# Holding GpSimd's first weight splits behind a juncture until the second half's sums of squares instead of the first half's

## The chip, the cores and the metric

One core of one Trainium2 chip runs the whole program. The metric is the device time of one execution in microseconds (us), as the median of several runs; smaller is better.

## The reference, cut to what matters

A sequence of 512 tokens of width 1024 goes through two attention layers (`first_block`) and then twice through FFN, token mixer, FFN (`second_block`). Each of these eight branches is normalised before and after and added to the stream:

```python
h = rms_norm(x, pre_norm[l]); proj = h @ w_in[l]
...
y = concatenate([oa, ob, om]) @ w_out[l]
x = x + rms_norm(y, post_norm[l])
...
h = swiglu(rms_norm_2(x, g[0]), ffn_w_in[layer, 0], ffn_w_out[layer, 0])
x = x + 0.5 * rms_norm_2(h, g[1])
h = token_mixer(rms_norm_2(x, g[2]), mix_w_in[layer], ...)
x = x + rms_norm_2(h, g[3])
```

All data is float32. `rms_norm` needs the sum of squares over all 1024 channels of a token.

## The kernel before, in words

**Layout.** The stream `XT` lies with channels on the partitions: 8 chunks of 128 channels by 512 tokens. Tokens are taken in two halves of 256 (`HALF`). Every float32 product is made of three matmuls of rounded parts: `mm3` (L353, L354, L355) multiplies high by high, high by low and low by high. So each weight tile is loaded (`wr`, L395, two buffers, 512 KB each), its high part is cast on ScalarE (`wh`, L419), and its low part, the difference, is made by GpSimd (`wl`, L421): one such *split* is 128x512, and a tile has two of them. A third tile can be loaded only when the two splits of the first have read their `wr`.

**A juncture** is where one branch ends and the next begins; seven of the eight ends have a next branch. Class `Join` does it: for each half `t` it waits for the norm of the branch's output (`scale`, `spread`), and then for each pair `i` of channel chunks runs `front(t, i)` and `back(t, i)`. `front` scales the output (VectorE L281, or L285 twice where a gain `gpost` is left to apply), adds it to the stream (VectorE L287), makes the next branch's high parts `xh` (ScalarE, L289, two), squares the pair (ScalarE L495) and lets GpSimd add the squares to `sacc` (`square2`: L498 once for the first pair, L501 twice for each other). `back` makes the low parts `xl` (VectorE L299, two), which read `XT` and `xh`. Four junctures end in an output projection (`gpost` is None: they begin near 344, 655, 1368 and 2456 us of the span); I call them *plain*. Three end an FFN (near 1030, 1746 and 2118 us), with `gpost`.

**Lead.** The next branch begins with `lead`: with weights that VectorE has already split, TensorE multiplies the two first units for half 0 (`run(0)`) and then for half 1 (`run(1)`), 32 `mm3` each. During `run(1)`, after 12 of them, it sums `sacc` over the partitions (`ss_matmul`, L473), VectorE makes the inverse root r of half 0 (`rsqrt`: nine instructions L364 to L372 on 128x2 values, each waiting for the one before), and after 18 more TensorE spreads r (`col_bcast`, L438), ScalarE copies it to `R` (L536), and VectorE scales the results (`evac`). The same is done for half 1 some `mm3` into the next unit. TensorE's order is fixed: a spread that has no r yet stops it.

**The gate.** The weights after the lead are split by GpSimd (`wload`, `wsplit`). Their program order is late, but the scheduler may place them early. `k.gate` holds the first 8 of them back: `behind` (L398) makes them stand behind a named GpSimd instruction in GpSimd's order.

```python
added = k.square2(k.pre[t], i, x)
if (t, i) == (0, 3):
    k.gate = [added, 8]
```

Of the kernel before, what the change touches and what calls it, by code (L numbers as in the profile page):

```python
# [210 lines left out]
class Join:  # L211
# [60 lines left out]
    def front(self, t, i):  # L272

        k, nc, put = self.k, self.nc, self.put
        v = nc.vector
        sl, c = HALF[t], slice(2 * i, 2 * i + 2)
        if t not in self.scratch:
            self.scratch[t] = (k.mm if t else k.sc)().rearrange("p (a n) -> p a n", a=2)
        s, P = self.scratch[t], self.P[t]
        if self.gpost is None:  # L280
            put(v.tensor_tensor(s, self.Y[:, c, sl], P[:, None, :].to_broadcast([128, 2, 256]), op=OP.mult))  # L281
        else:
            for e in range(2):
                j = 2 * i + e
                put(v.scalar_tensor_tensor(s[:, e], self.Y[:, j, sl], self.gpost[:, j:j + 1], P, op0=OP.mult, op1=OP.mult))  # L285
        x = k.XT[:, c, sl]
        put(v.tensor_tensor(x, x, s, op=OP.add))  # L287
        for j in (2 * i, 2 * i + 1):
            nc.scalar.activation(k.h[0][:, j, sl], k.XT[:, j, sl], AF.Copy, scale=k.gcol(self.nxt[0], j))  # L289
        added = k.square2(k.pre[t], i, x)  # L290
        if (t, i) == (0, 3):
            k.gate = [added, 8]

    def back(self, t, i):
# [1318 lines left out]
```

## Time and profile before

| | |
|---|---|
| median of 3 runs | 2847.77 us (2847.34 to 2848.65) |
| profiled execution, its own time | 2845.98 us |
| its span, first to last instruction | 2844.0 us |
| granted TensorE clock, mean | 0.992 |
| busy: TensorE matmul, VectorE, ScalarE, GpSimd | 2741.8, 1412.6, 1374.1, 1356.5 us |

The times in the trace are microseconds from the start of the span. A line such as `L421` is a line of the kernel; `[1.20 <-DVE xl L299]` means that the engine was idle for 1.20 us and that VectorE's instruction on `xl` ended that.

### The profile page before, as it was taken

The numbers are of one execution on the slowest core, as the hardware profiler recorded it, in microseconds if no ns is written. First come the engines' busy times: TensorE is split into PE (matmuls) and PEld (weight loads), VectorE is DVE, ScalarE is ACT, GpSimd is POOL, SyncE is SP. The second block draws the span as 40 slices with busy tenths as digits, with TensorE's granted clock in tenths as the row PEclk, the third lists the DMA queues.
The fourth block names the chain that finished last, engine by engine and source line by source line (L and its number), as shares of the span: only waits on it lengthen the run. The fifth ranks groups of instructions, "written<-read, shape, count | busy, mean of one in ns | idle before, by whom it ended". The sixth has DMA issues, their size and how long they took to land.

```text
span 2844.0 us, 42873 instructions
## 1 busy us (share of the span) xinstructions
PE 2741.8 (96%) x16080; PEld 2398.0 (84%) x16080; DVE 1412.6 (50%) x2988; ACT 1374.1 (48%) x2881; POOL 1356.5 (48%) x1327
## 2 busy tenths in 40 slices
PE   8999999999999999899999999999998899999998
PEld 8997899788888887898988888888887798888887
DVE  6589757986302266747630225312336747731132
ACT  5678547874333335657433334333334758433332
POOL 4553365424444455443544445444455543544545
PEclk9999999999999999999999999999999999999999
DMA  5111221112333222121223232233222120223332
GB/s 176 60 46 38 75 72 46 45 66 75 96 92 103 85 81 83 51 79 62 78 96 96 97 93 93 89 89 104 95 77 86 62 81 31 90 82 91 105 99 77
DMA packets 69280, 230.53 MB, mean 81 GB/s; under 512 B 8968, under 2 KB 11912, under 8 KB 68816
## 3 DMA queue, kind: packets, MB, share of 16 engines
q1 hardware_dynamic: 69072, 227.78, 24.5%
q8 instruction: 127, 2.08, 0.3%
q14 instruction: 81, 0.66, 0.1%
HBM read 225.51 MB, written 2.24 MB: 80 GB/s over the span
## 4 chain that ended last, share of the span: by engine, by line
PE 74%; DVE 15%; ACT 4%; issue 3%; POOL 2%; DMA 2%; SPq 0%; POOLq 0%; DVEq 0%; ACTq 0%
PE sc L354 11%; PE sc L353 11%; PE sc L355 11%; PE mm L355 11%; PE mm L353 11%; PE mm L354 11%; DVE xl L299 2%; PE sc L116 2%; PE tp L145 1%; DVE pl L149 1%; DVE XT L287 1%; DVE nm L192 1%; DVE E L204 1%; PE tp L817 1%; POOL wl L421 1%
## 5 line engine op out<-in xcount | busy, mean ns | idle before, releaser
L421 POOL TENSOR_TENSOR wl<-wr,wh 128x512 fp32r<-128x512 f32 x732 | 942.0, 1297 | 883.0 <-ACT wh L419 858.9
L419 ACT CAST wh<-wr 128x512 fp32r<-128x512 f32 x836 | 500.5, 612 | 722.8 <-PE sc L354 450.9
L354 PE MATMUL sc<-xl,wh 128*128 128x512 f32 (+1 forms) x1824 | 658.0, 361 | 16.3 <-DVE xl L299 16.2
L355 PE MATMUL sc<-xh,wl 128*128 128x512 f32 (+1 forms) x1824 | 654.5, 359 | 0.2 <-DVE wl L421 0.2
L353 PE MATMUL sc<-xh,wh 128*128 128x512 f32 (+1 forms) x1824 | 653.2, 360 | 0.0
L607 DVE TENSOR_TENSOR fg<-sc,R 128x512 f32<-128x512 f32 (+1 forms) x92 | 59.3, 644 | 747.6 <-PE sc L355 724.5
L354 PEld LDWEIGHTS sc<-xl,wh 128*128 128x128 f32 x1824 | 344.0, 189 | 72.1 <-DVE xl L299 20.7
L355 PEld LDWEIGHTS sc<-xh,wl 128*128 128x128 f32 x1824 | 344.2, 189 | 51.8 <-DVE wl L421 0.4
L353 PEld LDWEIGHTS sc<-xh,wh 128*128 128x128 f32 x1824 | 342.5, 189 | 51.5
L355 PE MATMUL mm<-ah,wl 128*128 128x512 f32 (+1 forms) x792 | 291.0, 367 | 6.5 <-POOL wl L421 6.5
L353 PE MATMUL mm<-ah,wh 128*128 128x512 f32 (+1 forms) x792 | 290.3, 367 | 1.9 <-ACT wh L419 1.9
L354 PE MATMUL mm<-al,wh 128*128 128x512 f32 (+1 forms) x792 | 289.3, 365 | 0.0
L353 PE MATMUL mm<-wh,xh 128*128 128x256 f32 x960 | 275.0, 286 | 0.0
L354 PE MATMUL mm<-wl,xh 128*128 128x256 f32 x960 | 273.2, 285 | 0.0
L355 PE MATMUL mm<-wh,xl 128*128 128x256 f32 x960 | 273.0, 284 | 0.0
L353 PE MATMUL mm<-xh,wh 128*128 128x512 f32 (+1 forms) x560 | 196.7, 353 | 10.5 <-DVE big L789 3.4
L355 PE MATMUL mm<-xh,wl 128*128 128x512 f32 (+1 forms) x560 | 194.8, 348 | 7.8 <-POOL wl L421 7.8
L354 PE MATMUL mm<-xl,wh 128*128 128x512 f32 (+1 forms) x560 | 193.9, 346 | 0.0
L354 PEld LDWEIGHTS mm<-wl,xh 128*128 128x128 f32 x960 | 184.1, 192 | 1.3
L353 PEld LDWEIGHTS mm<-wh,xh 128*128 128x128 f32 x960 | 183.9, 192 | 1.0
L355 PEld LDWEIGHTS mm<-wh,xl 128*128 128x128 f32 x960 | 184.0, 192 | 0.9
L355 PEld LDWEIGHTS mm<-ah,wl 128*128 128x128 f32 x792 | 149.2, 188 | 33.8 <-POOL wl L421 9.6
(348 smaller groups left out, 4878.1 us busy)
## 6 DMA issues: line engine op xcount, KB each, us to landing
wr<-in_ffn_in_dram SPq DMA_DIRECT2D x176, 512.0 KB, 3.3
wr<-in_ffn_out_dram SPq DMA_DIRECT2D x64, 512.0 KB, 3.6
wr<-in_mix_in_dram SPq DMA_DIRECT2D x56, 512.0 KB, 3.3
wr<-in_w_in_dram SPq DMA_DIRECT2D x48, 512.0 KB, 3.3
wr<-in_ffn_out_dram SPq DMA_DIRECT2D x32, 384.0 KB, 3.1
wr<-in_w_out_dram SPq DMA_DIRECT2D x16, 512.0 KB, 3.3
wr<-in_mix_out_dram SPq DMA_DIRECT2D x16, 512.0 KB, 3.3
Mb<-Md SPq DMA_DIRECT2D x16, 256.0 KB, 3.1
```

Of the source, the lines that this page charges most:

```text
L116: nc.tensor.matmul(sc[:, e], q, kk[:, :n], start=j == 0, stop=j == len(self.K) - 1)
L145: nc.tensor.transpose(p[:, j * per + e], E[i + e][:, j * 128:(j + 1) * 128], self.k.ident)
L149: nc.vector.tensor_tensor(pl[:, :nk, sl], pv, ph[:, :nk, sl].bitcast(F32), op=OP.subtract)
L192: nc.vector.tensor_reduce(nm, sc, axis=AX.X, op=OP.max, negate=True)
L204: nc.vector.scalar_tensor_tensor(E[tb, 0], E[tb, 1], cc[:, i:i + 1], E[tb, 0], op0=OP.mult, op1=OP.add)
L299: self.put(self.nc.vector.scalar_tensor_tensor(lo, k.XT[:, j, sl], k.gcol(self.nxt[0], j), hi.bitcast(F32), op0=OP.mult, op1=OP.subtract))
L353: mm(out, lhs[0], rhs[0], start=start, stop=False, skip_group_check=shared)
L354: mm(out, lhs[0], rhs[1], start=False, stop=False, skip_group_check=shared)
L355: mm(out, lhs[1], rhs[0], start=False, stop=stop, skip_group_check=shared)
L419: nc.scalar.copy(hi[:, :m], raw[:, c:c + m])
L421: ins = eng.tensor_tensor(low[:, :m], raw[:, c:c + m], hi[:, :m].bitcast(F32), op=OP.subtract)
L607: nc.vector.tensor_tensor(g, ps[0], R[:, sl], op=OP.mult)
```

## The change

The gate is set by the last sum of the second half instead of the last sum of the first half. The number of splits that it holds (8) stays.

```diff
         added = k.square2(k.pre[t], i, x)
-        if (t, i) == (0, 3):
+        if (t, i) == (1, 3):
             k.gate = [added, 8]
```

The scheduler then orders GpSimd and ScalarE otherwise; TensorE's order is the same row for row, and VectorE's differs by one pair of rows elsewhere.

GpSimd, second juncture (attention to FFN, 655 us). `sacc` of L498 and L501 are the sums of squares, `wl` the splits:

```order
 L501 TENSOR_TENSOR sacc<-sacc,sq 128x256 x4
-L421 TENSOR_TENSOR wl<-wr,wh 128x512 x4
-L498 TENSOR_TENSOR sacc<-sq 128x256
-L501 TENSOR_TENSOR sacc<-sacc,sq 128x256 x2
-L421 TENSOR_TENSOR wl<-wr,wh 128x512 x2
-L501 TENSOR_TENSOR sacc<-sacc,sq 128x256 x4
-L421 TENSOR_TENSOR wl<-wr,wh 128x512 x35
+L498 TENSOR_TENSOR sacc<-sq 128x256
+L501 TENSOR_TENSOR sacc<-sacc,sq 128x256 x6
+L421 TENSOR_TENSOR wl<-wr,wh 128x512 x41
```

Four splits stood in front of the second half's first sums and two more in the midst of them; now all of that half's seven sums come first, and the splits follow in one row. The other six junctures change in the same way.

ScalarE, third juncture (FFN to mixer, 1030 us). `xh` and `sq` are the pairs of the second half, `wh` the casts, `R` the copy of the spread r:

```order
 L495 ACTIVATE sq<-XT 128x512
-L419 CAST wh<-wr 128x512 x2
 L289 ACTIVATE xh<-XT,gains 128x256 x2
 L495 ACTIVATE sq<-XT 128x512
```

and a few rows on, at the copy of r:

```order
 L495 ACTIVATE sq<-XT 128x512
 L536 COPY R<-tp 128x256
-L419 CAST wh<-wr 128x512
+L419 CAST wh<-wr 128x512 x3
 L536 COPY R<-tp 128x256
```

The two casts of the third weight tile stood between the second half's pairs; now they stand behind the first copy of r. In the plain junctures one or two casts of that tile now stand right in front of that copy.

## Rows read from the trace of the kernel before

**Rows 1.** The page's first part: busy time of each engine, share, instructions.

```profile
PE 2741.8 (96%) x16080; PEld 2398.0 (84%) x16080; DVE 1412.6 (50%) x2988; ACT 1374.1 (48%) x2881; POOL 1356.5 (48%) x1327
```

**Rows 2.** Waits of TensorE over the span: us in total, times, longest us.

```profile
PE sc L354 <- DVE xl L299: 16.2, 21, 1.3
```

**Rows 3.** Timeline, GpSimd, second juncture (plain): start, us, instruction, count, idle before.

```profile
672.46 5.38 POOL L421 TENSOR_TENSOR wl<-wr,wh 128x512 fp32r<-128x512 f32 x4
677.80 0.91 POOL L498 TENSOR_TENSOR sacc<-sq 128x256 f32<-128x256 f32 x1
...
683.08 3.57 POOL L501 TENSOR_TENSOR sacc<-sacc,sq 128x256 f32<-128x256 f32 x4
```

**Rows 4.** Timeline, VectorE, same juncture: low parts and the chain for r.

```profile
667.08 0.88 DVE L299 SCALAR_TENSOR_TENSOR xl<-XT,gains,xh 128x256 fp32r<-128x256 f32 x2 [0.58 <-ACT xh L289]
...
675.47 2.64 DVE L299 SCALAR_TENSOR_TENSOR xl<-XT,gains,xh 128x256 fp32r<-128x256 f32 x2
...
679.36 1.36 DVE L299 SCALAR_TENSOR_TENSOR xl<-XT,gains,xh 128x256 fp32r<-128x256 f32 x2
...
681.96 4.09 DVE L299 SCALAR_TENSOR_TENSOR xl<-XT,gains,xh 128x256 fp32r<-128x256 f32 x4
685.97 0.15 DVE L364 TENSOR_SCALAR rnx<-tp 128x2 f32<-128x2 f32 x1
...
687.88 0.16 DVE L372 SCALAR_TENSOR_TENSOR r<-rnt,r 128x2 f32<-128x2 f32 x1
```

**Rows 5.** Timeline, TensorE, same juncture: two waits and the spread of r.

```profile
676.74 0.38 PE L354 MATMUL sc<-xl,wh 128*128 128x256 f32 x1 [1.20 <-DVE xl L299]
...
683.47 0.39 PE L354 MATMUL sc<-xl,wh 128*128 128x256 f32 x1 [0.43 <-DVE xl L299]
...
688.49 0.38 PE L438 MATMUL tp<-ident,r 128*128 128x128 f32 x2
```

**Rows 6.** Timeline, ScalarE, same juncture: third weight tile's casts, copy of r.

```profile
678.48 1.14 ACT L419 CAST wh<-wr 128x512 fp32r<-128x512 f32 x2 [1.46 <-DMA wr<-in_ffn_in_dram]
...
688.90 0.37 ACT L536 COPY R<-tp 128x256 f32<-128x256 f32 x1 [4.36 <-PE tp L438]
```

**Rows 7.** Timeline, VectorE, third juncture (FFN to mixer): low parts, end of r.

```profile
1047.52 2.73 DVE L299 SCALAR_TENSOR_TENSOR xl<-XT,gains,xh 128x256 fp32r<-128x256 f32 x2
...
1051.81 2.37 DVE L299 SCALAR_TENSOR_TENSOR xl<-XT,gains,xh 128x256 fp32r<-128x256 f32 x2
...
1060.29 0.16 DVE L372 SCALAR_TENSOR_TENSOR r<-rnt,r 128x2 f32<-128x2 f32 x1
```

**Rows 8.** Timeline, GpSimd, third juncture: its last two sums.

```profile
1057.43 1.63 POOL L501 TENSOR_TENSOR sacc<-sacc,sq 128x256 f32<-128x256 f32 x2 [0.53 <-ACT sq L495]
```

**Rows 9.** Timeline, TensorE, third juncture: first wait and the spread of r.

```profile
1048.87 0.39 PE L354 MATMUL sc<-xl,wh 128*128 128x256 f32 x1 [1.34 <-DVE xl L299]
...
1061.37 0.38 PE L438 MATMUL tp<-ident,r 128*128 128x128 f32 x2
```

**Rows 10.** Timelines of GpSimd and VectorE at the program's start.

```profile
57.90 2.54 POOL L421 TENSOR_TENSOR wl<-wr,wh 128x512 fp32r<-128x512 f32 x2 [1.63 <-ACT wh L419]
...
58.78 0.43 DVE L365 TENSOR_SCALAR r<-rnx 128x2 int32<-128x2 int32 x1
59.25 1.21 DVE L366 TENSOR_TENSOR rnt<-r 128x2 f32<-128x2 f32 x1
```

**Rows 11.** View of line L367: ns min/median/max, first and last start, shapes.

```profile
L367 DVE SCALAR_TENSOR_TENSOR rnt<-rnt,rnx x33: 160/160/163, 24.8 to 2834.1; 128x2 f32<-128x2 f32 x33
```

**Rows 12.** Timelines, VectorE and TensorE: half 1's r, first and third juncture.

```profile
382.06 0.16 DVE L372 SCALAR_TENSOR_TENSOR r<-rnt,r 128x2 f32<-128x2 f32 x1
...
383.10 0.38 PE L438 MATMUL tp<-ident,r 128*128 128x128 f32 x2
...
1065.13 0.16 DVE L372 SCALAR_TENSOR_TENSOR r<-rnt,r 128x2 f32<-128x2 f32 x1
...
1066.22 0.38 PE L438 MATMUL tp<-ident,r 128*128 128x128 f32 x2
```

## The prediction

> **What bounds the kernel now.** I began with the busy times: TensorE's matmuls fill 96% of the span [rows 1], so a change counts only where it makes TensorE stop, or no longer stop. The list of TensorE's waits comes next. Its first line is the wait of the lead's matmuls for VectorE's low parts: 16.2 us in 21 waits, three for each of the seven junctures [rows 2]. This change touches those junctures only, so I then read the timelines of one plain juncture (the second) and one behind an FFN (the third).
>
> In the second, four splits run on GpSimd from 672.46 us for 5.38 us, ahead of half 1's first sum [rows 3]. In that time VectorE's first two low parts take 2.64 us; the same two take 0.88 us when GpSimd is idle [rows 4]. TensorE waits 1.20 us for the first of them, and later 0.43 us for another [rows 5]. In the third juncture the pairs take 2.73 and 2.37 us [rows 7] and the first wait is 1.34 us [rows 9]. So an instruction of VectorE that reads two tiles of SBUF waits while a split runs. This is what the change can win. The reader should also see what lies behind it: the chain of small VectorE instructions that makes r ends at 688.04 us [rows 4], and TensorE takes r for the spread at 688.49 us [rows 5]. The slack is 0.45 us. In the third juncture it is 1061.37 − 1060.45 = 0.92 us [rows 7, 9]. Nothing splits in front of that chain today; only sums do.
>
> **The change part by part.** No instruction is added or removed. Six splits per juncture move behind half 1's sums, and with them the casts of the third weight tile.
>
> *Won: the lows, plain junctures.* Without splits the first low part takes its unhindered time, half of 0.88 us, and TensorE starts about 0.74 us sooner than 676.74 us (675.47 + 0.48 = 675.95 instead of 676.69). The second meets the 0.91 us first sum [rows 3], so the pair takes about 1.4 us, not 2.64. The next pair meets only sums, as now (1.36 us). Of the last four, which take 4.09 us against a full row of sums, I take some 2.8 us, since sums now start as soon as their squares are there and half of the lows miss them. That is 2.5 us altogether; the wait of 0.43 us goes, and TensorE would come to the spread at 688.49 − 0.74 − 0.43 = 687.3 us. Four times −1.2 us, if r is there.
>
> *Won: the lows behind an FFN.* There the first sum's squares are ready just before the first low part, so that one still waits, for a sum, not a split: I take 0.3 us won. The other two waits go: rows 2 leaves 16.2 − 4 × 2.1 = 7.8 us for nine waits (2.1 = 1.20 + 0.43 + a wait of 0.47 for half 0 that stays), 2.6 us for each of three junctures, 1.25 us of it behind the first wait of 1.34. TensorE would come to the spread at 1061.37 − 0.3 − 1.25 = 1059.8 us. Three times −1.55 us, if r is there.
>
> *Lost: r of half 0.* Here the moved splits land. Half 1's last sum ends at 683.08 + 3.57 = 686.65 us today [rows 3]; with the lows 2.5 to 2.7 us faster it ends near 684.0. Four splits stand ready behind it (two tiles loaded and cast long before) and start at once: at 5.38 / 4 with lows between, 1.27 each without [rows 3, 10], they run until 684.0 + 4 × 1.27 = 689.1 us. The chain for r starts with L364 some 0.7 us before the last sum ends, as today (685.97 against 686.65). What does one of its instructions pay behind a split? From below 0.16 us, its own time: L367 never took more than 163 ns in 33 executions [rows 11]. From above 1.21 us: at the program's start two splits ran back to back, and L365 waited for the first and L366, which started 40 ns after it, for the whole second [rows 10]. That is the same chain and the same split, and the next split starts before the instruction in front has left VectorE, so I take one split for one instruction: L365 ends with the last sum, L366 to L369 with the four splits, L370 to L372 follow at 0.2 us each. r is there at 689.1 + 0.6 = 689.7 us, and TensorE, which wanted it at 687.3, goes on at 689.7: 1.2 us later than the 688.49 of today.
>
> The Trainium skill (SBUF — State Buffer, "Who interferes with whom") says that a VectorE instruction with two SBUF inputs contends with a GpSimd instruction that reads SBUF, and that the loser is blocked for the whole instruction. By that rule L367, with its two inputs, pays like L366 and the sum is the one above; by the row of L367 alone it is −9.5 us, the first rival. No row here shows L367 behind a running split.
>
> *Why four, not six.* The third tile can be loaded only when the first tile's two splits have run, 2.5 us into the row; its load then takes 3.3 us (today they end near 675.2, half of the 5.38 us into their row, and the cast starts with the landing at 678.48 [rows 3, 6]) and its cast 0.6. It is there 6.4 us into the row, after r. In two junctures both of its casts and in two one of them stand before the copy of r to `R` on ScalarE, which then comes about 0.5 to 1.5 us later than r's spread alone would have it; that copy is waited for by VectorE, not by TensorE directly.
>
> *The same behind an FFN.* The sums end at 1057.43 + 1.63 = 1059.06 us today [rows 8]; with the lows 2.8 us faster at 1056.3. Four splits: 1061.3; r at 1061.8, against 1061.37: 0.4 us later.
>
> *r of half 1.* It follows in VectorE's order. Behind the mixers' leads r of half 1 ends at 1065.29 and is spread at 1066.22 [rows 12], 0.93 us of slack. The third tile's two splits now run in front of it: they cost two of its instructions up to 1.25 us each, and the splits' shift against TensorE is 0.4. I take 0.7 us lost twice, between 0.2 and 1.3. In the first juncture (slack 382.22 to 383.10 us, 0.88) the copy of r waits for two casts and sixteen small GpSimd instructions now follow the splits: 1.5 us lost, between 0.8 and 2.5. In the other four the spread stands 11 us behind (ten `mm3` of the FFN's first unit), and I cost it at nothing: VectorE's work on half 0 covers less than 8 us of that.
>
> *The weights themselves.* The first split is done at 685.3 us, and TensorE needs it at about 690.4 (two `mm3` behind the spread); it uses one split per 2.9 us (twelve 512-column matmuls), GpSimd makes one in 1.27. The third tile's first split is done near 691.8 and needed at 696. I cost this at nothing; the cover is 4 us and more, and without it TensorE would wait one split of 1.27 us.
>
> **The sum.** Plain: 4 × 1.2 = 4.8; behind an FFN: 3 × 0.4 = 1.2; half 1's r: 2 × 0.7 + 1.5 = 2.9. Together +8.9 us on the profiled execution's 2845.98, that is 2854.9; the median of the runs lies 1.8 us above that execution, so 2856.7 us.
>
> **The rivals.**
> - *Faster: r comes in time.* If the small instructions slip between two splits, r is there at about 685.5 us and TensorE does not wait: 4 × −1.2 and 3 × −1.55 make −9.5 us, 2838.3 us. For it: rows 11. Against it: rows 10. It decides at r before 687.3 us, which means that no more than two of the chain's instructions pay a split. I give it 9%.
> - *Both cancel.* If the chain starts about 1 us sooner than I think, or the row of splits later, fewer than four of its instructions meet splits, and each that does not saves 1.25 us per juncture; half of the loss gone in all seven is −4.4, and with half 1's r in time another −2.9: near +1.6 us, 2849.4 us. For it: the chain's start is my estimate to 0.5 us. Against it: the last sum and the chain's start hang on the same low parts. 24%, anywhere within 0.2%.
> - *More is lost.* If the third tile's splits also stand before r, or half 1's chain loses whole splits in more junctures, each adds up to 2.5 us for a juncture: +17.5 us, 2865 us. Against it: the load's 3.3 us. 6%.
> - *The change does nothing.* The order of instructions excludes it: the splits moved in all seven junctures.
>
> **How the numbers follow.** A measurement of this kernel can tell about 0.2%, 5.7 us, from no change. My forecast covers +5.7 to +15 us and gets 61%. With the last rival that makes slower 67%, the same 24%, faster 9%. The range leaves out the first rival and the tails: from 2848, where the gains and losses cancel, to 2865, where all seven junctures lose two and a half microseconds.
>
> **What the changed profile would show.** Right: no split between L498 and the last L501 of a juncture; low parts of the first pair at 1.0 to 1.4 us instead of 2.64 and 2.73; the wait for lows down from 16.2 to 5 us or less; L366 to L369 at 1.2 us each in all seven junctures, and a new wait of the spread L438 for L372, some 2 us, seven times. Wrong: no such wait, or L366 to L369 at 0.16 us; then the first rival holds. If L438 waits under 1 us, the second does. A wait of the first matmuls behind a lead for `wl` would show that the splits come too late as weights.

## The result and the profile after

The changed kernel takes 2865.93 us (median of 4 runs, 2861.28 to 2872.07) beside 2848.21 us (2847.34 to 2850.51) for the kernel before on the same chip: a ratio of 1.006, 95% interval [1.0048, 1.0071]. It is slower by 17.7 us. That is 0.9 us above the top of the predicted range; in three later runs, below, it was slower by 13.6, 15.1 and 13.8 us. The profiled execution is the longest of the four, 2872.07 us with a span of 2870.2; the one of before took 2845.98. The busy line and TensorE's waits of the changed kernel, to be held against [rows 1, 2]:

```profile
PE 2752.8 (96%) x16080; PEld 2408.5 (84%) x16080; DVE 1427.5 (50%) x2988; ACT 1373.9 (48%) x2881; POOL 1351.6 (47%) x1327
```

```profile
PE tp L438 <- DVE r L372: 20.2, 9, 2.8
...
PE sc L354 <- DVE xl L299: 6.3, 11, 0.9
```

The wait for the lows has fallen from 16.2 to 6.3 us, and a new one has taken its place: the spread L438 waits 20.2 us for r, nine times. Seven of these are half 0's, one a juncture, and two are half 1's, behind the leads of the second block's mixers. TensorE's busy time has grown by 11 us although it runs the same instructions: a first sign that some of them ran at a lower clock.

The second juncture shows the new wait. GpSimd, beside [rows 3]:

```profile
678.82 0.89 POOL L498 TENSOR_TENSOR sacc<-sq 128x256 f32<-128x256 f32 x1 [3.15 <-ACT sq L495]
...
685.51 1.88 POOL L501 TENSOR_TENSOR sacc<-sacc,sq 128x256 f32<-128x256 f32 x2 [1.02 <-ACT sq L495]
687.35 4.99 POOL L421 TENSOR_TENSOR wl<-wr,wh 128x512 fp32r<-128x512 f32 x4
693.92 2.54 POOL L421 TENSOR_TENSOR wl<-wr,wh 128x512 fp32r<-128x512 f32 x2 [1.58 <-ACT wh L419]
```

VectorE, beside [rows 4]:

```profile
678.65 1.35 DVE L299 SCALAR_TENSOR_TENSOR xl<-XT,gains,xh 128x256 fp32r<-128x256 f32 x2
...
683.82 2.15 DVE L299 SCALAR_TENSOR_TENSOR xl<-XT,gains,xh 128x256 fp32r<-128x256 f32 x4
685.88 0.15 DVE L364 TENSOR_SCALAR rnx<-tp 128x2 f32<-128x2 f32 x1
686.06 0.52 DVE L365 TENSOR_SCALAR r<-rnx 128x2 int32<-128x2 int32 x1
686.62 0.16 DVE L366 TENSOR_TENSOR rnt<-r 128x2 f32<-128x2 f32 x1
686.82 0.59 DVE L367 SCALAR_TENSOR_TENSOR rnt<-rnt,rnx 128x2 f32<-128x2 f32 x1
687.44 1.21 DVE L368 SCALAR_TENSOR_TENSOR r<-rnt,r 128x2 f32<-128x2 f32 x1
688.69 1.22 DVE L369 TENSOR_TENSOR rnt<-r 128x2 f32<-128x2 f32 x1
689.95 1.19 DVE L370 TENSOR_TENSOR rnt<-rnt,rnx 128x2 f32<-128x2 f32 x1
691.17 1.19 DVE L371 SCALAR_TENSOR_TENSOR rnt<-rnt 128x2 f32<-128x2 f32 x1
692.39 0.16 DVE L372 SCALAR_TENSOR_TENSOR r<-rnt,r 128x2 f32<-128x2 f32 x1
```

The lows are fast (1.35 us for the first pair, not 2.64). Four steps of the chain, L368 to L371, pay one split each: 1.2 us instead of 0.16. The chain of half 0 looks so at six junctures; at the fifth, where the sums end earlier, the four steps are L366 to L369. TensorE, beside [rows 5], at this juncture and at half 1's spread in the lead of the second block's first mixer (1066.22 us in the kernel before, without a wait):

```profile
692.70 0.41 PE L438 MATMUL tp<-ident,r 128*128 128x128 f32 x2 [2.41 <-DVE r L372]
...
1074.88 0.40 PE L438 MATMUL tp<-ident,r 128*128 128x128 f32 x2 [1.38 <-DVE r L372]
```

**Where the time went.** TensorE's order is the same in every kernel here (but for three matmuls of `fill` that change places with half 1's spread in the first juncture), so the start of the same instruction can be compared between two traces (a filler's own matmuls are left out). I cut each branch's end and beginning into parts and give what each profile adds to the kernel before's first trace, in us:

| profile | up to half 0's spread of r | from there to half 1's | last 14 us of the branches | rest | all |
|---|---|---|---|---|---|
| changed, the result | +5.6 | +9.4 | +7.1 | +3.9 | +26.0 |
| changed: again | +5.6 | +9.3 | +0.8 | −0.7 | +15.1 |
| changed: control | +5.7 | +7.4 | +3.7 | +0.2 | +17.0 |
| changed: changed_c | +5.7 | +8.6 | +1.1 | −1.7 | +13.7 |
| before_a | −0.1 | 0.0 | +0.9 | −0.2 | +0.6 |
| before_b | −0.1 | 0.0 | 0.0 | −0.3 | −0.3 |
| plain_only | +4.1 | +2.9 | +0.9 | +0.6 | +8.5 |
| ffn_only | +1.6 | +4.7 | +5.0 | +2.6 | +13.9 |
| stop_long | +10.5 | +1.7 | +1.5 | +0.4 | +14.2 |
| stop_short | +3.2 | +0.2 | +5.4 | −3.1 | +5.6 |
| fill | +5.1 | +3.3 | +5.8 | +8.7 | +22.9 |
| fill_ffn | +5.3 | +4.5 | +3.9 | −2.3 | +11.4 |
| fill_six | +5.4 | +4.8 | +6.0 | +0.9 | +17.0 |
| hold_for_r | −13.0 | +19.1 | +3.7 | +13.8 | +23.6 |
| hold_mix | −4.6 | +0.7 | +3.0 | +6.3 | +5.4 |
| gate_second | +14.6 | +9.4 | +1.2 | −4.2 | +20.9 |

The first column is a matter of tenths from execution to execution; in the changed kernel it is 1.0 us at each plain juncture and 0.4, 0.7 and 0.4 behind the FFNs. The second column holds two things. In front of the second block's mixers half 1's spread comes 1.5 to 1.6 us late each time (3.05 us together), with a wait of 1.3 to 1.4 us for r or, where a lower clock has taken that time already, without one. In the first juncture it comes about 1.0 us late, 1.6 with a lower clock in between. In the other four junctures, in front of an FFN, nothing waits there, and yet half 1's spread comes either 0.04 us late or 1.4 to 1.6 us. The view of windows shows two of these parts, the fourth and the fifth juncture's, in the run called control below (us, busy and instructions of PE, PEld, DVE, ACT, POOL, then the granted clock, DMA share and GB/s):

```profile
1410.85:1421.86 11.01, 11.01 (x54) 9.24 (x55) 6.28 (x17) 5.90 (x11) 5.78 (x5) 1.00 0.41 124
1784.15:1796.75 12.60, 12.60 (x55) 10.41 (x56) 6.90 (x17) 4.70 (x10) 5.94 (x5) 0.86 0.33 108
```

The same work takes 11.01 us with the clock granted in full (2.4 GHz) and 12.60 us where a part of it, right behind the spread's wait, was granted half (1.2 GHz). I call that part a half-clock stretch.

### The profile page after: what moved, and what is told of

It reads as the page before. It is cut to its first block, busy times and chain, and to the rows that moved or that the text cites. A ratio compares the mean times of both kernels' runs of the same rounds, so it can differ in the third digit from the quotient of the medians.

```text
span 2870.2 us, 42872 instructions
## 1 busy us (share of the span) xinstructions
PE 2752.8 (96%) x16080; PEld 2408.5 (84%) x16080; DVE 1427.5 (50%) x2988; ACT 1373.9 (48%) x2881; POOL 1351.6 (47%) x1327
## 4 chain that ended last, share of the span: by engine, by line
PE 73%; DVE 17%; ACT 4%; issue 2%; POOL 2%; DMA 1%; SPq 0%; POOLq 0%; DVEq 0%; ACTq 0%
PE mm L355 11%; PE mm L353 11%; PE mm L354 11%; PE sc L353 11%; PE sc L354 11%; PE sc L355 11%; DVE xl L299 2%; PE sc L116 2%; PE tp L145 1%; DVE pl L149 1%; DVE XT L287 1%; DVE nm L192 1%; DVE E L204 1%; PE tp L817 1%; POOL wl L421 1%
## 5 line engine op out<-in xcount | busy, mean ns | idle before, releaser
L354 PE MATMUL sc<-xl,wh 128*128 128x512 f32 (+1 forms) x1824 | 657.1, 361 | 6.5 <-DVE xl L299 6.3
L355 PE MATMUL sc<-xh,wl 128*128 128x512 f32 (+1 forms) x1824 | 655.5, 360 | 0.2 <-DVE wl L421 0.2
L354 PEld LDWEIGHTS sc<-xl,wh 128*128 128x128 f32 x1824 | 345.0, 189 | 59.8 <-DVE xl L299 8.8
L355 PEld LDWEIGHTS sc<-xh,wl 128*128 128x128 f32 x1824 | 345.1, 189 | 51.7 <-DVE wl L421 0.4
L355 PE MATMUL mm<-ah,wl 128*128 128x512 f32 (+1 forms) x792 | 292.5, 369 | 8.2 <-POOL wl L421 8.1
L354 PE MATMUL mm<-al,wh 128*128 128x512 f32 (+1 forms) x792 | 290.7, 367 | 0.0
L354 PE MATMUL mm<-wl,xh 128*128 128x256 f32 x960 | 273.7, 285 | 0.0
L355 PE MATMUL mm<-wh,xl 128*128 128x256 f32 x960 | 273.3, 285 | 0.0
L355 PE MATMUL mm<-xh,wl 128*128 128x512 f32 (+1 forms) x560 | 197.6, 353 | 7.8 <-POOL wl L421 7.8
L354 PE MATMUL mm<-xl,wh 128*128 128x512 f32 (+1 forms) x560 | 196.6, 351 | 0.0
L354 PEld LDWEIGHTS mm<-wl,xh 128*128 128x128 f32 x960 | 184.4, 192 | 1.3
L355 PEld LDWEIGHTS mm<-wh,xl 128*128 128x128 f32 x960 | 184.3, 192 | 0.9
L355 PEld LDWEIGHTS mm<-ah,wl 128*128 128x128 f32 x792 | 150.6, 190 | 35.6 <-POOL wl L421 11.5
```

The lines of the kernel that those rows point to most:

```text
L354: mm(out, lhs[0], rhs[1], start=False, stop=False, skip_group_check=shared)
L355: mm(out, lhs[1], rhs[0], start=False, stop=stop, skip_group_check=shared)
```

## The experiments

My theory after the result: r's lateness costs what the first column and the mixers show, and TensorE's stop there makes the chip take the clock to half behind it. The rivals: the half-clock stretches have another cause in the moved splits; or they cost nothing in the end. Cuts in the diffs are marked with `...`; `hold` is set in them until half 0 of a juncture has been dealt with.

The line numbers of a variant are up to 9 higher than the kernel before's; the names in a row tell which it is.

**again, control, changed_c: the changed kernel, unchanged.**

> The changed kernel once more, unaltered. Both theories: 2861 to 2872 us as before. Theory A (r is late behind four splits, TensorE stands still for 2.4 us at seven spreads, and after such a stop its clock is halved for a while): the profile shows seven waits of L438 for L372 of 2.4 to 2.9 us and two of about 1.4 us, and its time differs from the first profile's 2872.07 us by about 1.7 us for each half-clock stretch more or less. Theory B (the splits come too late as weights, and TensorE loses its time behind the leads waiting for wl): waits of mm L355 for wl grow by 10 us or more over the 14.4 us of the kernel before.

> The changed kernel once more, as the control for the filler beside it: 2858 to 2868 us, waits for half 0's r of 2.4 to 2.8 us at all seven junctures, and half-clock stretches right behind four or five of the seven.

> The changed kernel a fourth time, on the chip of the two runs of the kernel before: r's lateness gives 9 to 10 us at the same places as always; right behind the seven spreads two to five slow stretches of 1.5 us, and which ones is chance; branch ends 1 to 7 us above the kernel before's first trace.

Measured: 2860.78 us beside 2847.22, ratio [1.0036, 1.006]; 2865.05 beside 2849.94, [1.0044, 1.0069]; 2859.68 beside 2845.92, [1.0024, 1.0077]. Right behind half 0's spread a half-clock stretch began at 4 of 7 junctures in the result's profile, and at 5, 2 and 4 in these (for `control` I had expected four or five). The fifth and the seventh juncture have one in all four profiles, the sixth in none, the others in some. Theory B of `again` falls: TensorE's waits for splits in its `mm3` are 13.7 us there, beside 14.4 in the kernel before. So does the price that Theory A set: the profile of `again` has one such stretch more than the result's and is 11 us shorter. By the table these 11 us lie in the last 14 us of the branches (6.3) and in the rest (4.6), not behind the spreads.

**plain_only and ffn_only: the late hold at one kind of juncture.**

```diff
-        if (t, i) == (1, 3):
+        if (t, i) == ((1, 3) if self.gpost is None else (0, 3)):
```

and with (1, 3) and (0, 3) exchanged.

> The later gate at the four junctures behind output projections only; the three behind FFNs as before the change. Theory A: the spread 1.0 us later at each of four (4 us) and half-clock stretches of 1.6 us behind up to four of them: 2852 to 2860 us; no wait of L438 for r at the other three junctures and none for half 1's r behind the mixers' leads. Theory B gives no reason for a difference between the kinds; about four sevenths of 17 us, 2858 us, with waits for wl.

> The late hold only at the three junctures behind FFNs, the kernel before's hold at the four behind output projections. By the steps measured in the changed kernel's trace: 3 times 0.4 us net at half 0's spread, two waits of 1.4 us for half 1's r in the second mixers, 4 us in all, and 0 to 3 slow stretches of 1.5 us: 4 to 8.5 us above the kernel before, 2852 to 2857 us. Rival (the prediction's terms were right, 1.2 and 1.4 us, and there is nothing else): 2.6 us, 2851 us. Rival (only the plain junctures cost): within 1 us of the kernel before.

Measured: 2854.51 us beside 2847.22, [1.0017, 1.0038], and 2857.78 beside 2849.94, [1.0021, 1.0044]. Each kind is slower by itself, by 7.3 and 7.8 us, and the two add up to about what the changed kernel lost on the chips of these two runs, 13.6 and 15.1. The first lies in its expected range, and L438 waits for r at its four junctures alone. In ffn_only the first column is 1.6 us, as the steps of 0.4, 0.7 and 0.4 say, and the mixers' 3.05 are there; the time is 0.8 us above the expected top, and in this profile two stretches fell at branch ends, which I had not counted.

**stop_long and stop_short: a stop without the moved splits.** The kernel before, with 15 or 6 tiny VectorE instructions behind half 0's r, at the four junctures in front of an FFN (`toffn`).

```diff
-        self.rms(self.pre[t], self.r[:, 2 * t:2 * t + 2])
+        y = self.r[:, 2 * t:2 * t + 2]
+        self.rms(self.pre[t], y)
+        if self.hold and not t:
...
+                for _ in range(15 if self.toffn else 0):
+                    self.tc.keep_in_program_order(self.nc.vector.tensor_scalar(y, y, 1.0, None, op0=OP.mult))
```

> The kernel before, with 15 more tiny VectorE operations (r times 1, 128x2) behind half 0's r, at the four junctures that an FFN's first unit follows and nowhere else; GpSimd's splits stay where the kernel before has them. At 0.20 us each the r comes 2.95 us later, less the 0.45 us (three junctures) and 0.93 us (one) by which r was early in the trace of before: TensorE should stop for 2.5 us three times and 2.0 us once, 9.5 us in all, much as the changed kernel makes it stop. Theory (a stop of this length takes TensorE's clock down to half for 3.4 us behind it, which costs 1.6 us more in most places): half-clock stretches right behind two to four of the four spreads, and 12.7 to 16 us above the kernel before, 2860 to 2863 us. Rival 1 (the stop costs its own length and no more; the changed kernel's slow stretches come from something else that the held splits do): 9 to 10 us, 2857 us, and no new stretch at these places. Rival 2 (the work behind takes the stop up, since TensorE waits for weights there anyway): under 6 us.

> The same with 6 of the tiny operations: r comes 1.18 us later, TensorE should stop for 0.7 us three times and 0.25 us once, 2.4 us in all. Theory: stops this short leave the clock alone, since the kernel before has stops of 1.2 to 1.3 us at each juncture (its waits for the lows) and no slow stretch behind them: 2 to 3 us above the kernel before, 2849 to 2851 us. Rival (every stop at this place costs a slow stretch): 6 to 9 us. Rival (stops are taken up later): within 1 us of the kernel before.

Measured: 2859.85 us beside 2848.69, [1.0023, 1.0051]; and 2851.68, [1.0004, 1.0021]. The stops of the long one, in TensorE's waits:

```profile
PE tp L440 <- DVE r L539: 9.9, 4, 2.6
```

The stop alone, without one moved split, is enough for a half-clock stretch, but brought only one in four (behind 692.88 us, 1.6 us lost). So 11.2 us were lost, between the theory's 12.7 and the first rival's 9 to 10, and the interval does not choose. No later column wins the 10.5 us of the first one back, so the second rival falls. The short stops brought no stretch behind them, and the 3.0 us are as expected.

**fill, fill_ffn, fill_six: work in the stop.** The changed kernel with matmuls of no use in front of half 0's spread, 20 at all seven junctures, 22 at the four in front of an FFN, 28 at six.

```diff
         def out(t):
-            self.pre_rows(t)
+            p = None
+            if self.hold:
...
+                for _ in range(20):
+                    self.nc.tensor.matmul(p[:, 2:4].rearrange("p a b -> p (a b)"), self.wcol(w[0][0], slice(0, 128))[0],
+                                          xh[:, 0, HALF[0]], start=True, stop=True, skip_group_check=True)
+            self.pre_rows(t, p)
```

> The changed kernel with 20 matmuls of 128x256 (0.12 us each, 2.4 us; results unused) in front of half 0's spread of r at each of the seven junctures. They fill the time in which TensorE stood still. Theory A: waits for r of half 0 fall below 0.5 us each, the half-clock stretches right behind the spreads vanish, the delay itself stays: 2857 to 2862 us, faster than the changed kernel by 4 to 9 us although more is computed. If the clock had no part: 2866 us as the changed kernel, or more.

> The changed kernel with 22 matmuls of no use (128x256, results not read) just before half 0's spread, at the four junctures that an FFN's first unit follows; the mixers' junctures are left alone, and the order of the transfers on SyncE's queue is that of the changed kernel (the earlier filler at all seven places had put one more weight transfer ahead of the rope table at the first mixer, whose late landing cost that run about 6 us). TensorE then works through nearly all of its 2.4 us stop. Theory (the slow stretches come of the stop): none right behind these four spreads, and 3 to 6 us less than the changed kernel on this chip, 2855 to 2860 us. Rival (the stretches have another cause): the same number of them and the time of the changed kernel, 2861 to 2866 us.

> The changed kernel with 28 matmuls of no use (results not read) before half 0's spread at six of the seven junctures (all but the first mixer's, where more matmuls would put a weight transfer ahead of the rope table): enough to cover the whole stop. Theory (slow stretches come of the stops, about 1.5 us each): none behind these six, a wait for r under 0.3 us at each, and 4 to 7 us below the control run. Rival (what shows as slow stretches is made up later, or comes back elsewhere): no stretch there and yet the time of the control within 2 us. Rival (other cause): stretches as in the control.

Measured: 2866.42 us beside 2847.22, [1.0058, 1.0082]; 2862.24 beside 2848.69, [1.0032, 1.0057]; 2863.25 beside 2849.94, [1.0042, 1.0068]. All three times miss the theory and lie where the rivals put them. The traces bear out its other half: at none of the 17 filled spreads does a half-clock stretch begin, though the splits are moved as in the changed kernel, so the rival of another cause falls. The part from spread to spread of the fifth juncture, 12.60 us in the control run, takes 11.04 in fill_six:

```profile
1784.82:1795.86 11.04, 11.04 (x55) 9.27 (x56) 6.92 (x17) 4.83 (x10) 5.78 (x5) 1.00 0.35 117
```

The time is another matter. `fill_six` is 1.8 us below `control` in the medians, and the two profiles add the same 17.0 us in all: that is what the rival gave, by which the stretches are made up later or come back elsewhere. `control` had only two stretches behind spreads, so there were 3 us to win at the six; fill_six wins them (0.3 us in the second column at these four junctures, 3.3 in the control; what is left there, 3.0 in the mixers and 1.5 in the unfilled first juncture, is half 1's r and one stretch) and loses 2.3 us more at branch ends. Whether that loss is chance or belongs to the filler, no run shows, and a gain of 3 us can't be told in medians whose interval is 3.7 us to either side. That half-clock time costs in the end shows in another place: of the 17 executions of the changed kernel, the five with a mean granted clock of 0.990 or more took 2859.8 us on average, the eight at 0.989 took 2862.8, the four at 0.988 or less 2867.2. That holds for all half-clock time, not for the stretches behind spreads alone. In the run called fill another thing was lost: the filler put one weight transfer more ahead of the rope table on SyncE's queue, and VectorE, with half 1's r behind it, waited for the table in the first juncture's lead, which cost 6.0 us there:

```profile
386.23 0.24 DVE L1032 TENSOR_SCALAR lin<-tab,r 128x32 f32<-128x32 f32 x1 [4.34 <-DMA tab<-in_rope_dram]
```

**hold_for_r: the splits behind r.** No split may start before half 0's r is done: the eight are held behind a tiny GpSimd instruction that reads r.

```diff
     def pre_cols(self, t):
         self.rms(self.pre[t], self.r[:, 2 * t:2 * t + 2])
+        if self.hold:
...
+            ins = self.nc.gpsimd.tensor_tensor(seen, self.r[:, 0:2], self.r[:, 0:2], op=OP.add)
+            self.gate = [ins.ins, 8]
```

> The eight splits stand behind a tiny GpSimd instruction that reads r of half 0, so they start a little later still (some 0.2 to 0.5 us after r instead of with the end of the sums) but run against none of the nine instructions of that chain. Theory A: L366 to L372 take 0.16 us, no wait of L438 for r of half 0, TensorE reaches each spread 1.4 us (plain) or 2.1 us (behind an FFN) sooner than in the kernel before, 4 x 1.4 + 3 x 2.1 = 12 us, no half-clock stretch behind a spread: 2834 to 2840 us, faster than both. Theory B: splits still later, so 2866 us or more.

Measured: 2868.6 us beside 2847.22, [1.0062, 1.0086]: a miss on the other side, at the time that Theory B gave. The first half of Theory A holds: half 0's spread waits nowhere and TensorE is 13.0 us earlier there in sum, 1.5 and 2.3 us a juncture. With no split beside them, the steps that took 1.2 us in the changed kernel take 0.16:

```profile
688.62 0.16 DVE L368 SCALAR_TENSOR_TENSOR r<-rnt,r 128x2 f32<-128x2 f32 x1
688.81 0.16 DVE L369 TENSOR_TENSOR rnt<-r 128x2 f32<-128x2 f32 x1
```

All of the gain and more is lost behind it. ScalarE, VectorE and TensorE at the second juncture:

```profile
696.41 0.62 ACT L419 CAST wh<-wr 128x512 fp32r<-128x512 f32 x1 [4.32 <-DMA wr<-in_ffn_in_dram]
697.05 1.28 ACT L613 ACT_TABLE_LOAD   x1
698.35 0.72 ACT L613 ACTIVATE fg<-fg 128x256 f32<-128x256 f32 x2
```

```profile
698.80 0.76 DVE L615 TENSOR_TENSOR fu<-fu,fg 128x256 f32<-128x256 f32 x2 [5.25 <-ACT fg L613]
699.92 2.75 DVE L617 TENSOR_TENSOR al<-fu,ah 128x256 fp32r<-128x256 f32 x2 [0.36 <-ACT ah L616]
...
702.77 1.04 DVE L365 TENSOR_SCALAR r<-rnx 128x2 int32<-128x2 int32 x1
...
705.02 1.25 DVE L372 SCALAR_TENSOR_TENSOR r<-rnt,r 128x2 f32<-128x2 f32 x1
```

```profile
706.41 0.40 PE L438 MATMUL tp<-ident,r 128*128 128x128 f32 x2 [3.98 <-DVE r L372]
```

A split that comes later frees its `wr` later, so the next weight lands later. ScalarE works in order: the cast waits 4.32 us for it, with the silu (L613) behind it. VectorE waits 5.25 us for the silu, with half 1's chain behind it, and that chain meets the next splits. Half 1's r, which I had costed at nothing in these junctures, is now the one that is late: its spread comes 4.1 us later against half 0's than before here, 2.6 to 4.7 us in the five junctures that no second-block mixer follows. In or behind each of these five stops (2.5 to 4.5 us) the clock falls to half, and TensorE loses another 1.6 to 2.8 us in the next 25 us, 10.1 of the 13.8 us in the column "rest". The splits are not late as weights, as Theory B had it: the waits of L355 for them are 14.5 us beside 14.4; 2.1 us of waits for splits at L354 in the mixers are new.

**gate_second: the splits behind the second pair's sums.** `(1, 1)` in place of `(1, 3)`.

> The changed kernel with the eight splits held until the second of half 1's four pairs of sums of squares instead of the fourth: on GpSimd four splits come before the last four sums. By the changed kernel's trace of the second juncture they would run from about 682 to 687 us, beside half 1's last lows (about 1.5 us longer) and the start of half 0's r chain (one or two steps of 1.2 us instead of 0.2): r near 689.5 us, when TensorE arrives there at 690.3 us. Theory (what the change costs is the collision of the splits with the r chain and the stop that follows; what it saves, TensorE's arrival 1.4 to 2.1 us earlier per juncture, stays): no wait at half 0's spread or under 1 us, no slow stretch behind it, and 4 to 10 us faster than the kernel before, 2838 to 2844 us. Rival 1 (half 1's sums, now behind four splits, make half 1's r late instead, as a wait for r did): waits of 2 us or more at half 1's spread, 2850 to 2865 us. Rival 2 (the lows take up what the chain gains): as the changed kernel, 2860 us.

Measured: 2871.06 us beside 2848.69, [1.0063, 1.0088]: the second rival, and worse. VectorE at the second juncture:

```profile
683.20 4.63 DVE L299 SCALAR_TENSOR_TENSOR xl<-XT,gains,xh 128x256 fp32r<-128x256 f32 x4
687.76 0.15 DVE L364 TENSOR_SCALAR rnx<-tp 128x2 f32<-128x2 f32 x1
...
689.31 1.19 DVE L368 SCALAR_TENSOR_TENSOR r<-rnt,r 128x2 f32<-128x2 f32 x1
690.54 1.19 DVE L369 TENSOR_TENSOR rnt<-r 128x2 f32<-128x2 f32 x1
```

The lows take what the chain should have won (4.63 us for four instead of 2.15), the chain starts later, and two splits of the next tile still meet two of its steps. TensorE stops for 2.6 us at all seven spreads of half 0; six of the seven spreads are followed by a half-clock stretch.

**hold_mix: a version that might beat both.** The kernel before's hold at five junctures, hold_for_r's at the two in front of the second block's mixers (`mixes`); the diff is against the changed kernel.

```diff
-        if (t, i) == (1, 3):
+        if (t, i) == (0, 3) and not self.mixes:
...
+            self.gate = [ins.ins, 8]
```

> A version that may beat both kernels: the kernel before's hold at five junctures, and at the two that the second mixers follow the eight splits held behind a tiny GpSimd operation that reads half 0's r. In the run that held all seven junctures so, TensorE gained 2.0 and 1.6 us at these two places and lost 0.5 to 1.7 us again in the mixers, while the other five lost 2.6 to 6.3 us each. If that holds: 1 to 3 us faster than the kernel before, 2846 us beside 2848. Rival (the weights of the mixers come late by as much): within 1 us. Rival (half 1's r is late): 3 us or more slower.

Measured: 2852.74 us beside 2849.94, [1.0008, 1.0026]: slower by 2.8 us in the medians, and both the gain and the tie fall. TensorE is 2.3 us earlier at both spreads, and the mixers give it back, as the rival of late weights has it, and more: it waits there for splits, which the kernel before does not do at this place,

```profile
1092.76 0.38 PE L357 MATMUL sc<-wl,xh 128*128 128x256 f32 x1 [0.77 <-POOL wl L424]
1094.44 0.39 PE L357 MATMUL sc<-wl,xh 128*128 128x256 f32 x1 [0.71 <-POOL wl L424]
```

and 2.98 us for the casts of later weights at 1109.67 us, where the kernel before waits 1.44. No version here beats the kernel before.

**before_a, before_b: is the rest chance?** The kernel before, unchanged.

> The kernel before, unchanged, profiled again: to see what its own executions differ by at the places where the other runs lost time that the change does not explain (the last 14 us before each juncture, and the mixers' middles). Theory (those differences are chance): slow stretches or late waits at one to three of the seven branch ends, 1 to 4 us there together, as in the run with the short stop. Rival (the kernel before never has them, and a stop anywhere brings them): branch ends within 0.5 us of the first trace in sum. No new stretch right behind a spread by either.

> The same kernel once more; the same expectation as for the run before it.

Measured: 2846.5 and 2846.14 us beside 2845.92, [0.9991, 1.0014] and [0.9988, 1.0011]. No stretch behind any spread, as expected, and none at a branch's end either: 0.9 and 0.0 us there. The theory of chance in every execution falls. But the branch ends do not follow the change: the changed kernel adds 0.8 to 7.1 us there, and stop_short, which moves no split, 5.4.

## Why the prediction was wrong

**What came as predicted.** The lows: 1.35 us for the first pair, the wait for lows at 6.3 us (I had said 5 or less). The chain: four steps at 1.2 us each; in six junctures they are L368 to L371, not L366 to L369, because the last sum still ran beside L367. The weights themselves: TensorE's waits for splits are 15.9 us beside 14.4. *Lost: r of half 0* was put at 4 × 1.2 + 3 × 0.4 = 6.0 us and measured 5.6 to 5.7, in four profiles: 4 × 1.0, 0.4, 0.7 and 0.4. The stop that goes with it is 2.4 to 2.9 us long, since TensorE arrives earlier; the part of it by which TensorE is earlier costs nothing by itself. The rule of the Trainium skill (SBUF — State Buffer, "Who interferes with whom") that the loser waits for the whole instruction was the one to go by: L369 and L370, with two SBUF inputs, took 1.22 and 1.19 us where the unhindered step takes 0.16. With it the first rival fell, that r comes in time.

**The term that was mis-sized.** *r of half 1*, 2 × 0.7 + 1.5 = 2.9 us. In front of the second block's mixers it is 1.5 each. Two instructions of VectorE pay a split there, about 1.05 us each above their own time. In the result's profile they are in the sixth juncture L366 and L372, in the third L366 and L1219, a product with a table that stands between L371 and L372 and takes 0.24 us in the kernel before:

```profile
1071.26 1.20 DVE L366 TENSOR_TENSOR rnt<-r 128x2 f32<-128x2 f32 x1
...
1073.38 1.29 DVE L1219 TENSOR_SCALAR tr<-tabd,r 128x32 f32<-128x32 f32 x1
```

With the prediction's own 0.4 us of shift and 0.93 us of slack that is 2 × 1.05 + 0.4 − 0.93 = 1.6 us; it had two instructions, at up to 1.25 us each, and then took 0.7 us without giving a reason. In the first juncture the loss is about 1.0 us instead of 1.5. Together 4.1.

**The step that failed.** Of the four junctures in front of an FFN the prediction said that half 1's spread stands 11 us behind, and put it at nothing. For r that is right: nothing waits there. But the sum has no term for TensorE's clock. It counted a stop by how much later the spread comes, and took the work behind the stop at full speed. Over ten profiles TensorE stopped 50 times for 2.1 to 2.9 us at half 0's spread (the four of the changed kernel, plain_only, ffn_only, stop_long, gate_second, and the unfilled ones of fill_ffn and fill_six): right behind 28 of them the granted clock was half for a while. With work in the stop (0 to 1.2 us of it left), 0 of 17; at stop_short's stops of under 1 us, 0 of 4; in the three profiles of the kernel before, 0 of 21, nor in hold_for_r's seven, where nothing stops. Each costs 1.4 to 1.6 us where no wait behind it hides it, as the traces have it at half 1's spread (no median shows it by itself): 3.3 to 4.8 us per execution in the four junctures in front of an FFN. With the two terms above that is 5.7 + 4.1 + 3.3 to 4.8 = 13.1 to 14.6 us, where 13.6, 15.1 and 13.8 us were measured in three runs and 17.7 in the first. Of the first run's 17.7 us some 3 stay without a cause here; by the table its profile loses 11.0 us at the branch ends and in the rest.

The kernel before waits 1.2 us for the lows [rows 5] with no stretch behind it; the prediction did not ask what a stop twice as long does. The trace of the kernel before could have raised the question: it has six half-clock stretches, at the program's two ends and in the second block's mixers, and each begins in a stop of 2.3 to 3.9 us or within 2.5 us behind one. One of these stops, and the windows of 10 us before and behind it:

```profile
1172.29 0.40 PE L1409 MATMUL sc<-mv,Ch 128*128 128x258 f32 x1 [2.30 <-DVE W L1390]
```

```profile
1162.29:1172.29 10.00, 7.22 (x51) 6.45 (x50) 7.03 (x31) 7.94 (x27) 4.62 (x5) 1.00 0.08 28
1172.29:1182.29 10.00, 9.75 (x50) 8.98 (x50) 7.06 (x25) 5.22 (x16) 5.02 (x5) 0.66 0.23 79
```

The sign and the places of the waits were right; the loss was forecast 9 us too small for the first run, 5 to 6 for the others.

**What stays open.** The last 14 us of the branches, 0.8 to 7.1 us in the changed kernel, much of it half-clock stretches there (three in the result's profile, none in two others). They are not in the kernel before's three profiles, and they also come in kernels that stop TensorE elsewhere. That a new stop anywhere moves where the clock falls is a guess; no run here tests it. That a filler gains time is not shown either: it takes the stretches away, but the medians can't tell 3 us. And why the clock falls behind one stop of 2.4 us and not behind the next is not known: in the four profiles of the changed kernel the first four junctures differ each time. The five longest of the 50 stops, 2.8 to 2.9 us, each had one; so did 23 of the other 45.

## What to carry to other kernels

In this kernel the GpSimd splits cost least beside long VectorE instructions, and most beside a chain of tiny dependent ones: each low part pays for about one split, the chain of nine for each split that runs while it does, and it is the chain that TensorE stands still for. Moving such work later moves its price, since the buffers that it frees come later too: ask which transfer, which cast and what behind that cast in its queue will be late next. Where TensorE is as busy as here (96%), cost a new stop of the length seen here, 2.1 to 2.9 us, at more than its length: 1.5 us more behind every second one.

## What had not been expected of the hardware

The granted clock fell to half behind 28 of 50 stops of 2.1 to 2.9 us, and only in part at the same places in each execution of the same kernel. The Trainium skill (TensorE: Matmul & The Clock Gate, "HAM oscillation — how this bites in real kernels") says that a wait for data can take TensorE to half rate, so that the next work starts there; its case is a wait longer than the work between two waits. The traces agree, show it for stops much shorter than the work around them, and show that at this length it happens behind about every second stop.

A VectorE instruction on 128x2 values takes as long beside a 128x512 split as a low part on 128x256 does. The chain's four steps take 1.19 to 1.22 us each, in a row beside four splits in a row (4.99 us); two low parts beside splits take 2.64 us [rows 4]. The forecast had this from one instruction of 1.21 us; that it holds for four in a row is new.
